# A difference of two activation blocks moved from DVE to POOL at the entry of the MLP

## The chip, the cores and the metric

The kernel runs on one core of a Trainium2 chip. A core has five engines that matter here: PE (the matrix engine; PEld is its loading of weights), DVE (VectorE), ACT (ScalarE), POOL (GpSimd) and SP, which only issues DMAs. Each runs its own queue of instructions in order, and they meet at semaphores. The metric is the device time of one execution in microseconds (us), the median of several.

## The reference: what is computed

One decoder layer with D_MODEL 1024, 512 tokens and one batch, all in float32: a modulated RMSNorm, two attention branches with gates and an output projection, then a second modulated RMSNorm `h2` and a gated MLP with a causal convolution, and a final RMSNorm. The change lies at the entry of the MLP:

```python
def _conv_ffn(h, w_up, conv_w, conv_b, w_down):
    u = h @ w_up
    a, g = jnp.split(u, 2, axis=-1)
    ...
    return (jax.nn.gelu(a, approximate=False) * g) @ w_down
```

`w_up` is 1024 x 5632 (two halves of 2816 columns), `h` is 512 x 1024.

## The kernel before

**A product in three matmuls.** A float32 matrix is used as a rounded high part and the low part that is left. ACT makes the high part (a cast), DVE the low part (source minus high part), and PE forms high x high, high x low and low x high. So each operand costs an ACT cast and a DVE subtraction before its matmuls can start.

**The MLP's first product by seven products.** `w_up` and the normalised input are cut into 2 x 2 blocks, and the eight block products are replaced by seven products of sums of blocks, in the manner of Strassen and Winograd. The kernel names them p1, m5, m6, p2, m7, p3 and p4. The blocks of the normalised, transposed input are `b11`, `b21`, `b12`, `b22`, each of 128 partitions x 4 x 256 (1024 float32 per partition). `b12` and `b22` are the two halves of one tile that the profile calls `braw`. The sums of input blocks that the products need are formed once: `t1n = b11 - b12`, then `t1n = -t1n - b22`, `b12 = b22 - b12` and `b21 = -t1n - b21`. Their high and low parts go to `tt[0]` to `tt[3]`, which the text calls t1 to t4 (tile `t` in the profile): `hi_t(i, ...)` is ACT's cast into `tt[i]`, L1275, and `lo_t(i, ...)` is DVE's subtraction, L1278. m5 uses t1, m6 uses t2, m7 uses t3 and p4 uses t4. p3 uses `b22` itself, whose high part is `bh[:, 2]` and whose low part is `bl[:, 2]` (L1407).

**The weights.** `w_up` is worked through in pairs of 128-column blocks, numbered J. For each J and each product, `sum_w` (DVE, L1087) forms the sum of weight blocks where m6 and p3 need one, `cast_w` (ACT, L1093) makes the high part `whi` and `low_w` (DVE, L1097) the low part `wlo`; three buffers of each kind go round. Some sums come from the DMA itself: SP issues the first load of a tile, and POOL issues a second load that adds to it (L1065). Raw loads go to SP's queue (L1063).

**The order around the change.** From the last steps of the output projection to the first slots of J = 2 the order of the instructions on PE, DVE, ACT and POOL is the order in which the program is written (a manual schedule); nothing is reordered by a planner. `mul_slot(J, name)` is 24 matmuls of one product (L1152), `behind(J, name)` takes its result out of PSUM: ACT copies for p1, m5 and m6, DVE additions for p2, m7 (L1192), p3 (L1194) and p4. `mod_one` (L1255 on DVE, L1257 on ACT) writes the blocks `b..` from the transposed rows with scale and shift. `conv_bias`, `conv_taps` (L1163, L1164) and `conv_gelu` are the convolution and its GELU. L1397 is the second form of `t1n`.

**POOL's queue here** holds four small powers for the RMSNorm (L173, of 128x1), then three adding loads of weights (one for J = 0, two for J = 1), and then the adding loads of later J; it does no other arithmetic in this stage.

Of the kernel before, what the change touches and what calls it, by code (L numbers as in the profile page):

```python
# [53 lines left out]
def kernel(  # L54
# [22 lines left out]
    nc = tc.nc  # L77
# [1055 lines left out]
    def psum(J, name):  # L1133
        if name in ("m5", "p3"):
            b, h = bV, J % 2
        elif name == "p2":
            b, h = bX, J % 2
        else:
            b, h = (bU0, bU1)[J % 2], J // 2 % 2
        return [b[u][:, h * H : (h + 1) * H] for u in range(2)]  # L1140
# [33 lines left out]
    def behind(J, name):  # L1174
        o = [] if name == "c22" else psum(J, name)
        g2 = g22[:, J % 2] if name in ("m5", "m7", "c22") else None
        if name == "p1":
            av[J] = big.tile([P, 2, S], F32, tag=("hhB", "hlB")[J % 2], name=f"a{J}")
        a = av[J]
        lo, hi = slice(0, H), slice(H, S)  # L1180
        for u in range(2):
            cc = grow(2 * J + u)
            if name == "p1":
                nc.scalar.copy(a[:, u, lo], o[u])
            elif name == "m5":
                nc.scalar.copy(g2[:, u], o[u])
            elif name == "m6":
                nc.scalar.copy(a[:, u, hi], o[u])
            elif name == "p2":
                nc.vector.tensor_add(a[:, u, lo], a[:, u, lo], o[u])  # L1190
            elif name == "m7":
                nc.vector.scalar_tensor_tensor(g2[:, u], g2[:, u], -1.0, o[u], ALU.mult, ALU.subtract)  # L1192
            elif name == "p3":
                nc.vector.tensor_add(a[:, u, hi], a[:, u, hi], o[u])  # L1194
            elif name == "p4":
                nc.vector.scalar_tensor_tensor(cc[:, lo], o[u], -1.0, cc[:, lo], ALU.mult, ALU.mult)
            elif name == "c22":
                nc.vector.tensor_mul(cc[:, hi], cc[:, hi], g2[:, u])
        if name == "p4":
            nc.vector.tensor_sub(grow(2 * J)[:, hi], grow(2 * J + 1)[:, hi], grow(2 * J)[:, hi])  # L1200
# [58 lines left out]
    def ks(g):  # L1259
        return slice(2 * (g % 2), 2 * (g % 2) + 2)  # L1260
# [13 lines left out]
    def hi_t(i, src, q=slice(0, 4)):  # L1274
        nc.scalar.copy(tt[i][:, 0, q], src[:, q])  # L1275
# [10 lines left out]
    V, q0, q1 = nc.vector, ks(0), ks(1)  # L1286
# [67 lines left out]
    b12, b22 = bt[:, 0], bt[:, 1]  # L1354
# [8 lines left out]
    def grow(j):  # L1363
        return gT[j // 4][:, j % 4]
# [31 lines left out]
    for q in (q0, q1):  # L1396
        V.scalar_tensor_tensor(t1n[:, q], t1n[:, q], -1.0, b22[:, q], ALU.mult, ALU.subtract)  # L1397
        hi_t(1, t1n, q)
    behind(0, "p1")
    nc.scalar.copy(bh[:, 2], b22)  # L1400
    low_w(0, "m6")
# [4 lines left out]
    cast_w(0, "p3")  # L1406
    V.tensor_sub(bl[:, 2], b22, bh[:, 2].bitcast(F32))  # L1407
    behind(0, "m5")
    V.tensor_sub(b12, b22, b12)
    hi_t(2, b12)  # L1410
    low_w(0, "p3")
    mul_slot(0, "p3")
# [404 lines left out]
```

## Time and profile before

| What | Value |
|---|---|
| median of 3 runs | 703.3 us (701.72 to 703.88) |
| profiled execution | 702.35 us, span 700.5 us |
| PE busy | 682.6 us, 97% of the span |
| DVE busy | 573.1 us, 82% |
| ACT busy | 375.1 us, 54% |
| POOL busy | 82.4 us, 12% |
| mean granted clock of PE | 0.995 |
| L1409 on DVE | 1 instruction of 1216 ns, at 378.8 us |

The span reaches from the first to the last instruction; the execution's time holds some 1.9 us more. Busy times are sums over the span and overlap between engines. A line such as L1409 is the line of the kernel before; a helper's line is shared by all its callers, so the time in the span tells which call it is.

### The profile page before, as it was taken

The numbers are of one execution on the slowest core, as the hardware profiler recorded it, in microseconds if no ns is written. First come the engines' busy times: TensorE is split into PE (matmuls) and PEld (weight loads), VectorE is DVE, ScalarE is ACT, GpSimd is POOL, SyncE is SP. The second block draws the span as 40 slices with busy tenths as digits, with TensorE's granted clock in tenths as the row PEclk, the third lists the DMA queues.
The fourth block names the chain that finished last, engine by engine and source line by source line (L and its number), as shares of the span: only waits on it lengthen the run. The fifth ranks groups of instructions, "written<-read, shape, count | busy, mean of one in ns | idle before, by whom it ended". The sixth has DMA issues, their size and how long they took to land.

```text
span 700.5 us, 11253 instructions
## 1 busy us (share of the span) xinstructions
PE 682.6 (97%) x4203; PEld 595.0 (85%) x4203; DVE 573.1 (82%) x1100; ACT 375.1 (54%) x666; POOL 82.4 (12%) x100
## 2 busy tenths in 40 slices
PE   6999999999999999999999999999999999999995
PEld 5777777777788888888889999999999999888884
DVE  5999886887985656663589999888888999979996
ACT  4646666454552333332468656655555666656664
POOL 3000000000001000000030111112111102540300
PEclk9999999999999999999999999999999999999998
DMA  9995454354535676239717788786889738997903
GB/s 313 289 273 159 149 152 151 98 173 121 140 102 160 207 232 185 91 99 281 251 39 144 151 200 199 174 209 184 209 213 217 173 129 219 191 198 196 166 1 120
DMA packets 115862, 121.81 MB, mean 174 GB/s; under 512 B 4383, under 2 KB 93280, under 8 KB 115808
## 3 DMA queue, kind: packets, MB, share of 16 engines
q1 hardware_dynamic: 96894, 95.09, 43.4%
q0 software_dynamic: 18720, 25.73, 22.0%
q8 instruction: 33, 0.54, 0.3%
q10 hardware_dynamic: 194, 0.28, 0.1%
q14 instruction: 21, 0.17, 0.1%
HBM read 118.97 MB, written 2.11 MB: 173 GB/s over the span
## 4 chain that ended last, share of the span: by engine, by line
PE 75%; DVE 13%; DMA 4%; ACT 4%; issue 2%; SPq 0%; POOL 0%; POOLq 0%; ACTq 0%
PE up L1152 26%; PE dc L1761 13%; DMA ra<-in_w_ada_dram 4%; PE a L332 3%; PE pgd L119 2%; PE oc L1208 2%; PE oc L1212 2%; PE pgd L121 2%; PE oc L1209 2%; PE pgd L120 2%; PE pga L119 2%; PE pga L121 2%; PE pga L120 2%; DVE arow L778 1%; DVE m_wlo L1097 1%
## 5 line engine op out<-in xcount | busy, mean ns | idle before, releaser
L1152 PE MATMUL up<-t,m_whi 128*128 128x256 f32 x528 | 96.2, 283 | 0.0
L1152 PEld LDWEIGHTS up<-t,m_whi 128*128 128x128 f32 x528 | 82.3, 192 | 0.0
L1152 PE MATMUL up<-t,m_wlo 128*128 128x256 f32 x264 | 74.7, 284 | 0.5 <-DVE m_wlo L1097 0.5
L1152 PE MATMUL up<-bh,p_wlo 128*128 128x256 f32 x232 | 65.6, 283 | 0.1
L1152 PE MATMUL up<-bh,p_whi 128*128 128x256 f32 x232 | 65.6, 283 | 0.0
L1152 PE MATMUL up<-bl,p_whi 128*128 128x256 f32 x232 | 65.6, 283 | 0.0
L778 DVE SCALAR_TENSOR_TENSOR arow<-ra,cs,arow 128x512 f32<-128x512 f32 x56 | 41.9, 749 | 21.0 <-DMA ra<-in_w_ada_dram 20.5
L1152 PEld LDWEIGHTS up<-t,m_wlo 128*128 128x128 f32 x264 | 50.6, 192 | 0.9 <-DVE m_wlo L1097 0.9
L1152 PEld LDWEIGHTS up<-bh,p_wlo 128*128 128x128 f32 x232 | 44.5, 192 | 0.3 <-DVE p_wlo L1097 0.3
L1152 PEld LDWEIGHTS up<-bl,p_whi 128*128 128x128 f32 x232 | 44.5, 192 | 0.0
L1152 PEld LDWEIGHTS up<-bh,p_whi 128*128 128x128 f32 x232 | 44.5, 192 | 0.0
L1065 POOL DMA_DIRECT2D s<-in_w_up_dram x21 | 27.0, 1360 | 143.1 <-DMA s<-in_w_up_dram 54.2
L1097 DVE TENSOR_TENSOR m_wlo<-s,m_whi 128x1024 fp32r<-128x1024 f32 x31 | 37.7, 1217 | 0.9 <-ACT m_whi L1093 0.9
L1093 ACT CAST m_whi<-s 128x1024 fp32r<-128x1024 f32 x31 | 32.4, 1047 | 9.6 <-DVE s L1087 6.2
L1152 PE MATMUL up<-t,p_whi 128*128 128x256 f32 x176 | 32.3, 284 | 0.5 <-DVE pairs L1192 0.5
L173 POOL TENSOR_TENSOR r<-ms,mhalf 128x1 f32<-128x1 f32 (+1 forms) x16 | 12.7, 796 | 133.1 <-DVE ms L171 74.1
L795 POOL DMA_DIRECT2D mod_rows<-row x8 | 5.1, 642 | 197.4 <-ACT row L794 197.4
L1152 PEld LDWEIGHTS up<-t,p_whi 128*128 128x128 f32 x176 | 27.4, 192 | 0.7 <-issue 0.7
L698 ACT ACTIVATE sd<-sd,dmx 128x128 f32<-128x128 f32 (+3 forms) x32 | 17.7, 557 | 19.0 <-DVE dmx L690 18.8
L1159 ACT ACTIVATE gT<-a,cv 128x512 f32<-128x512 f32 x22 | 17.7, 813 | 17.7 <-DVE a L1194 17.3
L1093 ACT CAST p_whi<-wa 128x1024 fp32r<-128x1024 f32 x18 | 18.7, 1041 | 12.0 <-PE up L1152 7.2
L1152 PE MATMUL up<-t,p_wlo 128*128 128x256 f32 x88 | 24.9, 283 | 0.0
(473 smaller groups left out, 2053.6 us busy)
## 6 DMA issues: line engine op xcount, KB each, us to landing
ra<-in_w_ada_dram SPq DMA_DIRECT2D x32, 512.0 KB, 3.9
wa<-in_w_up_dram SPq DMA_DIRECT2D x22, 512.0 KB, 4.0
s<-in_w_up_dram SPq DMA_DIRECT2D x21, 512.0 KB, 4.7
s<-in_w_up_dram POOLq DMA_DIRECT2D x21, 512.0 KB, 6.9
adaw<-in_w_ada_dram SPq DMA_DIRECT2D x16, 512.0 KB, 5.4
w<-in_w_in_dram SPq DMA_DIRECT2D x12, 512.0 KB, 3.9
a<-in_w_up_dram SPq DMA_DIRECT2D x11, 512.0 KB, 4.7
b<-in_w_down_dram SPq DMA_DIRECT2D x10, 512.0 KB, 3.8
```

The source lines that it names most:

```text
L119: nc.tensor.matmul(o, lh, rh, start=start, stop=False)
L120: nc.tensor.matmul(o, lh, rl, start=False, stop=False)
L121: nc.tensor.matmul(o, ll, rh, start=False, stop=stop)
L332: nc.tensor.matmul(acc6[i], lhs[:, i * P : (i + 1) * P], rhs[k], start=k == 0 and p == 0, stop=last and p == 2)
L698: exp = nc.scalar.activation(pm[m], pm[m], AF.Exp, bias=mx[:, m : m + 1], scale=slope, accum_out=lsum[:, m : m + 1])
L778: nc.vector.scalar_tensor_tensor(ac, r[:, a], cc, ac, ALU.mult, ALU.add)
L1065: nc.gpsimd.dma_start(dst, upblock(*blk), accum_op=ALU.add)
L1093: nc.scalar.copy(W[J, name][0], R[J, SRC[name]])
L1097: nc.vector.tensor_sub(lo, R[J, SRC[name]], hi.bitcast(F32))
L1152: nc.tensor.matmul(o[u], w[:, k, cu], b[:, k], start=name in ("p1", "m5", "p2") and k == 0 and x == 0, stop=k == 3 and x == 2, skip_group_ ...
L1159: nc.scalar.activation(grow(j), av[J][:, u], AF.Identity, bias=cv[:, 66 + j : 67 + j], scale=cv[:, 44 + j : 45 + j])
L1761: nc.tensor.matmul(bank2[u][:, sl], a[:, q, cu], b[:, q, sl], start=first_mm and x == 0, stop=last_mm and x == 2, skip_group_check=name no ...
```

## The change

The subtraction that forms `b12 = b22 - b12` is issued on POOL (`nc.gpsimd`) in place of DVE (`V` is `nc.vector`), and its place in the written order is earlier: behind the loop that forms the second `t1n`, ahead of the low weights of m6 and the weight sum of p3. Operands, shapes and result stay what they were. PE, ACT and SP keep their instructions and their order. ACT's cast `hi_t(2, b12)` now waits for POOL. In POOL's queue the new instruction stands behind the three adding loads for J = 0 and 1 and ahead of the first adding load for J = 2.

```diff
     for q in (q0, q1):
         V.scalar_tensor_tensor(t1n[:, q], t1n[:, q], -1.0, b22[:, q], ALU.mult, ALU.subtract)
         hi_t(1, t1n, q)
+    nc.gpsimd.tensor_sub(b12, b22, b12)
     behind(0, "p1")
     nc.scalar.copy(bh[:, 2], b22)
     low_w(0, "m6")
...
     cast_w(0, "p3")
     V.tensor_sub(bl[:, 2], b22, bh[:, 2].bitcast(F32))
     behind(0, "m5")
-    V.tensor_sub(b12, b22, b12)
     hi_t(2, b12)
     low_w(0, "p3")
     mul_slot(0, "p3")
```

## The prediction

> **What bounds the kernel now.** I read the page's busy shares first (PE 97%, DVE 82%, POOL 12%), then busy time by stretches around the edited line, then the list of waits there, then the chain of work that ended last, and at the end the timelines of DVE, ACT and POOL. The times below are microseconds from the start of the span. Busy time by stretches; after the length, the columns are PE, PEld, DVE, ACT, POOL (instructions in brackets), granted clock, DMA share, GB/s:
>
> ```profile
> 372.00:380.00 8.00, 8.00 (x69) 8.00 (x68) 8.00 (x11) 5.18 (x9) 0.00 (x0) 1.00 0.81 180
> 380.00:412.00 32.00, 30.99 (x252) 30.14 (x250) 30.85 (x43) 21.98 (x33) 5.10 (x4) 1.00 0.67 144
> 412.00:450.00 38.00, 37.94 (x316) 37.95 (x317) 33.88 (x51) 22.06 (x32) 5.13 (x4) 1.00 0.87 198
> ```
>
> DVE has no gap between 372 and 380, and about a microsecond in the next 32. PE loses its time in the second row only: from 412 on it is full (to 600 as well). So whatever DVE gains or loses between 372 and 412 reaches PE there, and PE carries it to the end unchanged. The waits of 372 to 412 name what PE waited for (engine, line, then what it waited on, us in total, times, longest):
>
> ```profile
> PE up L1152 <- DVE pairs L1192: 0.5, 1, 0.5
> PEld up L1152 <- DVE m_wlo L1097: 0.5, 1, 0.5
> ...
> PEld up L1152 <- DVE p_wlo L1097: 0.3, 1, 0.3
> ...
> PE up L1152 <- DVE m_wlo L1097: 0.3, 1, 0.3
> ```
>
> All are waits for DVE. Matmuls of this stage start 0.12 apart; at the four stalls the starts are 0.38 apart (380.80 to 381.18), 0.55 (384.03 to 384.58), some 0.77 (to 390.88) and, at 412.06, a wait of 0.20. That is 0.26 + 0.43 + 0.65 + 0.2, about 1.5 us: no relief of DVE here can give more. The removed subtraction and its neighbours on DVE (start, duration, line, out<-in):
>
> ```profile
> 371.75 1.29 DVE L1278 TENSOR_TENSOR t<-s_t,t 128x512 fp32r<-128x512 f32 x2
> 372.96 1.28 DVE L1397 SCALAR_TENSOR_TENSOR s_t<-s_t,braw 128x512 f32<-128x512 f32 x2
> 374.16 1.22 DVE L1097 TENSOR_TENSOR m_wlo<-s_t,m_whi 128x1024 fp32r<-128x1024 f32 x1
> ...
> 377.64 1.22 DVE L1407 TENSOR_TENSOR bl<-braw,bh 128x1024 fp32r<-128x1024 f32 x1
> 378.77 1.22 DVE L1409 TENSOR_TENSOR braw<-braw 128x1024 f32<-128x1024 f32 x1
> 379.91 1.22 DVE L1097 TENSOR_TENSOR p_wlo<-s_t,p_whi 128x1024 fp32r<-128x1024 f32 x1
> ```
>
> L1409 is the instruction that goes. Every DVE instruction shown reads two operands from SBUF, and each starts about 0.08 before its forerunner ends.
>
> **Part 1, DVE loses L1409.** Start to start it costs 379.91 - 378.77 = 1.14 us of an engine that has no gap. Without it p_wlo (L1097) ends at 379.99 instead of 381.13, and its matmul, due at 380.92, no longer waits. The second stall (m_wlo of m7, DVE end 384.53) is due 383.4 against a PE that comes at 383.9: gone. The third shrinks: DVE's end moves from 391.06 to 389.9, PE arrives at 389.5. What is late next is again DVE, at 412, where it is 1.14 earlier. Full worth: -1.1 us.
>
> **Part 2, POOL gains one subtraction of 128x1024.** Its order on POOL is behind three accumulating weight loads and ahead of the next one. The last of the three issues is over at 368.3; the next load is issued at 388.55, after a wait of 20.2 for a DMA. So nothing queued on POOL's queue notices an instruction of a few microseconds; SP's queue is not touched. The subtraction waits for DVE's L1383 (ended 369.4) and for ACT's last write of b22 (L1257, which ends at 371.84). It is ready at 371.9, not at 378.8.
>
> **Part 3, ACT's rounding of b12 (hi_t(2), L1275) waits for POOL instead of DVE.** ACT started it at 380.02 after 0.68 of idle time; ACT itself is free at 379.35. POOL therefore has 379.35 - 371.9 = 7.4 us of cover. Behind it on ACT stand the rounding of m7's weights, two copies of m6 and hi_t(3); they lose nothing as long as the cover holds, so this wait costs nothing. Past the cover each microsecond of POOL delays hi_t(2), then DVE's low part of t3 and m7's matmuls, one for one.
>
> **Part 4, POOL beside DVE.** The trace has no POOL subtraction, but has rows in which the two engines meet:
>
> ```profile
> 350.09 0.57 POOL L173 TENSOR_TENSOR r<-ms,mhalf 128x1 f32<-128x1 f32 x1 [28.44 <-DVE ms L171]
> 354.32 0.94 POOL L173 TENSOR_TENSOR r<-ms,mhalf 128x1 f32<-128x1 f32 x1 [3.67 <-DVE ms L171]
> ```
>
> ```profile
> 2.88 0.52 DVE L233 TENSOR_SCALAR cs<-cs 128x8 f32<-128x8 f32 x1 [2.02 <-ACT cs L232]
> ...
> 5.33 0.17 DVE L241 TENSOR_SCALAR cols<-cols 128x8 f32<-128x8 f32 x1
> ...
> 354.16 0.69 DVE L1293 TENSOR_TENSOR early<-wa,early 128x512 fp32r<-128x512 f32 x1
> ```
>
> ```profile
> 2.83 0.55 POOL L148 IOTA ddf<- 128x512 f32 x1
> 3.34 0.39 POOL L145 TENSOR_SCALAR_AFFINE_SELECT dsw<-dsw 128x256 f32<-128x256 f32 x1
> 3.70 0.61 POOL L149 TENSOR_SCALAR_AFFINE_SELECT ddf<-ddf 128x512 f32<-128x512 f32 x1
> ```
>
> The same POOL instruction takes 0.57 with DVE idle and 0.94 when it starts inside a DVE instruction with two SBUF inputs: it ends 355.26, which is 0.41 after DVE's end at 354.85. At 359.80 it does so again (0.40 after). The other way round, DVE's 128x8 at 2.88 took 0.52 instead of 0.17 and ended at 3.40, just after POOL's IOTA (2.83 to 3.38). So each can hold the other up to the other's end. At 695.25 POOL's power started in the first of two adjoining two-input DVE products (L1683, 695.03 and 695.36, 0.42 each) and ended at 695.85, 0.40 after the first: it was let in between the two. I therefore expect POOL to start at 372.43, when the first L1278 ends, and DVE's second L1278 to wait until POOL has read.
>
> How long is that? One-input selects give (607 - 395) ns / 256 = 0.83 ns per element, 0.85 us for 1024; a POOL instruction let in has 0.40 besides (above). Low end: both inputs stream at once, 0.40 + 0.85 = 1.25 us. High end: read, read and write one after the other, 0.40 + 2.55 = 2.95. I take the middle, two passes, 0.40 + 1.70 = 2.1 us: it is nearest to the selects, which read one operand and write one in 0.83 ns, with the second operand added. A lower end, no hold at all, is a rival below; the power rows (1.03 for 128x4 against 0.55: 0.16 us per element, 164 us for 1024) I leave out as the work of a power, with 2 in 100.
>
> The Trainium skill, GPSIMD Engine Reference, section "Performance versus the Vector engine", gives 4497 ns for a two-input add of 2048 elements; half of it is an estimate of 2.25 us, and the sum would be +1.1 instead of +1.0.
>
> DVE is thus 2.1 later from 372.43 and 2.1 - 1.14 = 1.0 later from L1409's place on. In between PE has slack: m5's matmuls start at 374.92 and need the second half of t1's low part only at the eighth (375.8; it comes at 375.1); m6 needs its first low half at 377.92, and gets it at 378.1 (375.98 + 2.1). p3 needs p_wlo, which comes at 382.1: PE restarts 1.0 later than before, and so at 384.58, 390.88 and 412.06.
>
> **Sum.** -1.14 + 2.1 = +1.0 us. The profiled execution took 702.35 (span 700.5 and 1.85 around it), 0.95 below the median of 703.3; 703.35 against its own time, 704.3 against the median. With the ends of part 4: +0.1 to +1.8, 703.4 to 705.1.
>
> **Rivals.**
> - *POOL does not hold DVE at all* (faster). For it: POOL's power of 128x4 (181.75 to 182.94) had DVE's two-input L704 start inside it at 182.61 and take its usual 0.61. Against it: that power has only four elements to read, and had read them. Decides if DVE's rows at 372 to 375 keep 0.68. Then part 1 alone: -1.1, 702.2.
> - *POOL is not let in* while DVE's two-input instructions follow each other without a gap. For it: there is no gap until DVE itself needs b12; against it: 695.25. DVE would run p_wlo and L1413 to 381.1 and stop; POOL 381.1 to 383.2, hi_t(2) to 384.3, low part of t3 to 385.5, m_wlo of m7 to 386.7 instead of 384.53: +2.2, and hi_t(3), behind two more ACT jobs, some 0.3 more. 705.5 to 705.8.
> - *POOL is much slower than its selects*, above 3.3 us, under DVE's traffic. Every microsecond of hold counts in full: 4 us gives +2.9, 706.2.
>
> By the Trainium skill, SBUF — State Buffer, section "Who interferes with whom", a VectorE instruction with two SBUF inputs and a GpSimd instruction that reads SBUF exclude each other for the whole instruction, and whichever issues first blocks the other. By that rule the forecast's hold is right and moving the work gives nothing; the trace shows the wait in both directions, but no long two-input POOL read.
>
> **How the numbers follow.** 0.3% (2.1 us) is about what a measurement of this kernel can tell from no change. Hold of about one subtraction: 0.50, mostly within 0.3%, 0.12 of it beyond for its upper end and the spread of the medians. Not let in: 0.22, on the bound, 0.17 of it beyond. Much slower POOL, the power's rate included: 0.12, all beyond. No hold: 0.16, 0.08 of it counted as beyond -0.3% because the medians' spread (701.72 to 703.88) can add a microsecond. Faster 0.08, same 0.51, slower 0.41. The range cuts the outer half of the no-hold case and the slowest POOL: 702.2 to 706.3; the likeliest case alone is 703.4 to 705.1.
>
> **What would show it.** POOL's L1399 starting at 372 to 372.5 and lasting 1.3 to 3; one DVE instruction near 372.4 (L1278 or L1397) stretched by as much; no L1409 on DVE; hi_t(2) starting near 381 without a wait for POOL; p_wlo's end at 382.1 relative to the same start; PE's wait before p3 over 1 us; PE full after 412. Wrong if the DVE rows beside POOL are unstretched (then faster), if POOL starts only at 381, or if PE loses time behind 412.

## The result, and the profile after

The changed kernel takes 703.95 us in the median of 19 runs (703.16 to 705.8), the kernel before 702.54 us in as many (701.72 to 704.57): a ratio of 1.0016, 95% interval 1.0008 to 1.0023. That is +1.1 us (0.6 to 1.6): less than the 0.3% that the prediction took for the least that can be told from no change, and still clear of no change, since there are 19 runs of each. The profiled execution of the changed kernel took 703.97 us with a span of 702.0 us, beside 702.35 and 700.5 before.

The profile after, busy time by stretches, same columns as before (PE, PEld, DVE, ACT, POOL, clock, DMA share, GB/s):

```profile
372.00:380.00 8.00, 7.84 (x65) 7.64 (x64) 8.00 (x9) 3.91 (x7) 2.77 (x1) 1.00 0.75 156
380.00:412.00 32.00, 30.67 (x249) 29.82 (x248) 30.86 (x43) 22.19 (x34) 5.13 (x4) 1.00 0.61 143
412.00:450.00 38.00, 37.80 (x315) 37.59 (x314) 33.88 (x49) 21.96 (x32) 5.13 (x4) 1.00 0.85 198
```

DVE is as full as it was and does less: 9 instructions in 372 to 380 in place of 11. POOL shows 2.77 us where it had none. The timelines of the changed kernel show where the time went (start, duration, line, out<-in). POOL's:

```profile
372.28 2.77 POOL L1399 TENSOR_TENSOR braw<-braw 128x1024 f32<-128x1024 f32 x1 [3.61 <-ACT braw L1257]
```

And DVE's:

```profile
372.11 3.50 DVE L1278 TENSOR_TENSOR t<-s_t,t 128x512 fp32r<-128x512 f32 x2
375.53 1.28 DVE L1397 SCALAR_TENSOR_TENSOR s_t<-s_t,braw 128x512 f32<-128x512 f32 x2
...
380.21 1.21 DVE L1408 TENSOR_TENSOR bl<-braw,bh 128x1024 fp32r<-128x1024 f32 x1
381.40 1.23 DVE L1097 TENSOR_TENSOR p_wlo<-s_t,p_whi 128x1024 fp32r<-128x1024 f32 x1
```

The pair of L1278 took 1.29 us before and takes 3.50 now: +2.21. Taken singly, the first ran 372.11 to 372.79 as ever, and the second 372.71 to 375.61, 0.56 after POOL's end at 375.05. POOL was ready inside the first and got in behind it; the second then waited until POOL was done. L1409 is gone, so from the first L1278 to p_wlo's start it is 9.29 us (372.11 to 381.40) against 8.16 before (371.75 to 379.91): +1.13. PE's timeline of the changed kernel, what it waited for in the last brackets:

```profile
378.60 0.38 PE L1152 MATMUL up<-t,m_whi 128*128 128x256 f32 x1 [0.16 <-DVE t L1278]
...
382.68 0.39 PE L1152 MATMUL up<-bh,p_wlo 128*128 128x256 f32 x1 [0.49 <-DVE p_wlo L1097]
...
386.09 0.39 PE L1152 MATMUL up<-t,m_wlo 128*128 128x256 f32 x1 [0.28 <-DVE m_wlo L1097]
...
392.38 0.47 PE L1152 MATMUL up<-t,p_whi 128*128 128x256 f32 x2 [0.49 <-DVE pairs L1192]
```

The last two waits are those of before, of the same length; the first is new and the second longer. The first matmul of m5 and the last stall, before:

```profile
374.92 0.40 PE L1152 MATMUL up<-t,m_whi 128*128 128x256 f32 x2
...
412.06 0.38 PE L1152 MATMUL up<-t,m_wlo 128*128 128x256 f32 x1 [0.20 <-DVE m_wlo L1097]
```

The same two, after:

```profile
375.28 0.40 PE L1152 MATMUL up<-t,m_whi 128*128 128x256 f32 x2
...
413.54 0.39 PE L1152 MATMUL up<-t,m_wlo 128*128 128x256 f32 x1 [0.20 <-DVE m_wlo L1097]
```

From the one to the other PE needed 412.06 - 374.92 = 37.14 us before and 413.54 - 375.28 = 38.26 now: +1.12, and after it PE is full in both. The rest of the two spans' difference of 1.5 us, 0.36, stood already at m5's first matmul, ahead of the change's place; it belongs to these two executions and not to the change.

ACT's rounding of b12 was never late. ACT's timeline of the changed kernel:

```profile
380.32 1.05 ACT L1093 CAST p_whi<-s_t 128x1024 fp32r<-128x1024 f32 x1 [1.36 <-DVE s_t L1087]
381.28 0.63 ACT L1186 COPY pairs<-up 128x256 f32<-128x256 f32 x2
381.80 1.06 ACT L1275 CAST t<-braw 128x1024 fp32r<-128x1024 f32 x1
```

L1275 has no idle time in front of it (0.68 before): b12 had been ready since 375.05.

### The profile page after: what moved, and what is told of

It reads as the page before. It is cut to its first block, busy times and chain, and to the rows that moved or that the text cites. A ratio compares the mean times of both kernels' runs of the same rounds, so it can differ in the third digit from the quotient of the medians.

```text
span 702.0 us, 11254 instructions
## 1 busy us (share of the span) xinstructions
PE 682.4 (97%) x4203; PEld 593.5 (85%) x4203; DVE 574.3 (82%) x1099; ACT 374.9 (53%) x666; POOL 85.2 (12%) x101
## 4 chain that ended last, share of the span: by engine, by line
PE 74%; DVE 15%; DMA 5%; ACT 3%; issue 2%; SPq 0%; POOL 0%; POOLq 0%; ACTq 0%; DVEq 0%
PE up L1152 26%; PE dc L1761 13%; DMA ra<-in_w_ada_dram 3%; PE a L332 2%; PE pgd L119 2%; PE oc L1208 2%; PE oc L1212 2%; PE pgd L120 2%; PE pgd L121 2%; PE oc L1209 2%; PE pga L119 2%; PE pga L121 2%; PE pga L120 2%; DVE m_wlo L1097 1%; DVE arow L778 1%
## 5 line engine op out<-in xcount | busy, mean ns | idle before, releaser
L1097 DVE TENSOR_TENSOR m_wlo<-s,m_whi 128x1024 fp32r<-128x1024 f32 x31 | 37.7, 1217 | 0.9 <-ACT m_whi L1093 0.9
```

The costliest lines, as they stand in the source:

```text
L1097: nc.vector.tensor_sub(lo, R[J, SRC[name]], hi.bitcast(F32))
```

## Experiments

The theory: the removed DVE instruction is worth about 1.1 us, and POOL's subtraction costs DVE the time for which POOL reads SBUF, about 2.2 us, because DVE's next instruction reads two operands from SBUF. Rivals: the cost is ACT's new wait or the moved order; it is a fixed price of each meeting; any POOL instruction, or any DVE instruction, is affected. Where not said otherwise, an edit is made to the kernel before.

**Each half of the change alone.** First the subtraction on no engine, so that b12 goes on unsubtracted:

```diff
-    V.tensor_sub(b12, b22, b12)
```

> The kernel before without the subtraction b12 = b22 - b12 on any engine (b12 goes on unsubtracted, so that part of the computation is left out; everything else is as before). It measures what the removed DVE instruction is worth alone. Hold theory (DVE's 1.14 us comes back, POOL's hold takes 2.2): about -1.1 us against before, PE waits before p3 and m7 gone, PE full after 412. Rival (the change is slower because something other than the hold was lost, and the removal is worth little): within 0.3 us of before.

Measured: 701.46 us against 702.38, ratio 0.9988 (0.9978 to 0.9997), so -0.8 us (-1.5 to -0.2). The times alone reach into the rival's 0.3 us; the trace decides below. Between m5 and 412 PE waits only twice, for `pairs` (0.3) and for `m_wlo` (0.2). Then the opposite, DVE's subtraction kept and a second one on POOL whose result nobody reads:

```diff
         hi_t(1, t1n, q)
+    nc.gpsimd.tensor_sub(fgb.rearrange("p (k n) -> p k n", n=256), b22, b12)
     behind(0, "p1")
```

> The kernel before with its DVE subtraction kept, and a POOL subtraction of the same two operands into a buffer that nobody reads, at the changed kernel's place. It measures the hold alone. Hold theory: one DVE L1278 at 372 stretched by about 2.2 us, +2.2 us against before, no wait of ACT for POOL. Rival (ACT's new wait for POOL, or the moved order, is what costs): no change, since nobody waits for this POOL instruction.

Measured: 704.33 us against 702.38, ratio 1.0028 (1.0018 to 1.0038), so +2.0 us (1.3 to 2.7). The timeline of DVE in this kernel:

```profile
371.40 3.50 DVE L1278 TENSOR_TENSOR t<-s_t,t 128x512 fp32r<-128x512 f32 x2
...
380.64 1.21 DVE L1410 TENSOR_TENSOR braw<-braw 128x1024 f32<-128x1024 f32 x1
381.77 1.22 DVE L1097 TENSOR_TENSOR p_wlo<-s_t,p_whi 128x1024 fp32r<-128x1024 f32 x1
```

And its longest wait of PE (us in total, times, longest):

```profile
PE up L1152 <- DVE p_wlo L1097: 1.6, 1, 1.6
```

The same 3.50 us, although no engine waits for this POOL instruction. So neither ACT's new wait nor the moved order is the cause; the meeting itself is. The halves add up: -0.8 + 2.0 = +1.2, and the change measured +1.1.

**What of POOL's work holds DVE.** POOL writes the idle buffer and reads nothing:

```diff
+    nc.gpsimd.memset(fgb, 0.0)
```

> The kernel before with a POOL memset of 128x1024 float32 into the same idle buffer at the same place in POOL's queue: it writes 1024 elements per partition and reads none. If POOL's reads are what holds DVE's two-input instructions: DVE rows beside it keep 0.68 and 1.22 us. If any long POOL instruction that writes SBUF holds them: one DVE row stretched by the memset's length, some 0.9 us.

One profiled run, 702.46 us. POOL in this kernel's timeline:

```profile
366.90 2.57 POOL L1399 MEMSET fgbr<- 128x1024 f32 x1
```

And DVE beside it:

```profile
368.34 1.28 DVE L1383 TENSOR_TENSOR s_t<-braw,braw 128x512 f32<-128x512 f32 x2
```

The memset needs no data and so started at 366.90, beside the issues of the adding loads (364.57 to 368.51), and ended at 369.47. The only two-input work of DVE in that span, the pair of L1383, kept its 1.28; the next, L1097, starts after it. When within its span the memset wrote can't be read from this, so it says less than the next one, a copy with one input:

```diff
+    nc.gpsimd.tensor_copy(fgb.rearrange("p (k n) -> p k n", n=256), b22)
```

> The kernel before with a POOL copy of b22 (128x1024 float32, one input) into the idle buffer at the same place. If the hold lasts as long as POOL reads, and two operands are read one after the other: a DVE row stretched by about half of the changed kernel's 2.2 us, 1.0 to 1.3. If the hold is a fixed price of meeting: 2.2 again. If one input holds nothing: 0.

One run, 702.54 us. POOL in this kernel's timeline:

```profile
371.33 1.43 POOL L1399 COPY fgbr<-braw 128x1024 f32<-128x1024 f32 x1 [3.58 <-ACT braw L1257]
```

And DVE beside it:

```profile
371.18 2.13 DVE L1278 TENSOR_TENSOR t<-s_t,t 128x512 fp32r<-128x512 f32 x2
```

The pair took 0.84 us more than its 1.29, a little under the 1.0 to 1.3 expected. A copy holds DVE too, and for less than half of the subtraction's 2.21: 0.82 ns per element against 2.16. The price is no fixed one, and a subtraction costs more than twice a copy. Whether that lies in the second operand alone is not shown, since the operation differs too. Nor do the runs separate POOL's reading from the whole of its instruction; only the memset bears on that, and weakly. Half of the subtraction, as an additional instruction:

```diff
+    nc.gpsimd.tensor_sub(fgb.rearrange("p (k n) -> p k n", n=256)[:, q0], b22[:, q0], b12[:, q0])
```

> The kernel before with its own subtraction kept and a POOL subtraction of the first 512 columns only, into the idle buffer, at the same place. Hold theory: one DVE row near 372 stretched by 1.1 us, half of the 2.2 of the full one, and some +1 us at the end, less what slack there is before p3. Rival (fixed price): 2.2 again.

It became ready a little earlier and met L1087 in place of L1278:

```profile
371.32 2.27 DVE L1087 TENSOR_TENSOR s_t<-s_t,wa 128x1024 f32<-128x1024 f32 x1
```

That is 2.27 us instead of 1.22, so +1.05, about half of 2.21 as expected. The one run took 703.99 us, 1.6 over the median before; by its time alone one run can't be told from the +1 expected. Then the changed kernel's subtraction in two halves:

```diff
-    nc.gpsimd.tensor_sub(b12, b22, b12)
+    for q in (q0, q1):
+        nc.gpsimd.tensor_sub(b12[:, q], b22[:, q], b12[:, q])
```

> The changed kernel with POOL's subtraction in two halves of 128x512, one behind the other. Hold theory (DVE waits for as long as POOL reads, 2.2 ns per element): the stretch of DVE's rows is 2.2 us in sum again, perhaps in two rows of 1.1 if DVE gets in between the halves; the time stays at some +1.1 us over before. Rival (a fixed price for each meeting of the two engines): the stretch doubles to 4.4, +3.3 us.

DVE's timeline in this kernel:

```profile
370.65 2.26 DVE L1087 TENSOR_TENSOR s_t<-s_t,wa 128x1024 f32<-128x1024 f32 x1
372.83 2.38 DVE L1278 TENSOR_TENSOR t<-s_t,t 128x512 fp32r<-128x512 f32 x2
```

Two rows are stretched, by 1.04 and 1.09, 2.1 in sum: DVE and POOL take turns, and twice as many meetings cost no more. One run took 703.62 us, +1.2 over before.

**Which DVE work is held.** An additional POOL subtraction, ready when DVE has a gap and then two instructions that read PSUM:

```diff
+    nc.gpsimd.tensor_sub(fgb.rearrange("p (k n) -> p k n", n=256), b21, bl[:, 1].bitcast(F32))
     load_s3(0)
```

> The kernel before with an additional POOL subtraction of 128x1024 (b21 minus the low part of p2's block, into an idle buffer) that becomes ready some 5 us earlier, when DVE has nothing to do for 0.6 us and then two instructions that read PSUM and no block from SBUF (L1255), before its next two-input instruction (L1383). If only DVE instructions with two SBUF inputs are held: POOL starts at about 366.7, both L1255 rows keep 0.54 us beside it, and the first L1383 is stretched to POOL's end at about 369, by some 0.7 us and not 2.2. If any DVE instruction is held by POOL's reads: L1255 stretched by 1.5 to 2 us. The three adding loads behind it on POOL are issued some 3 us later, which may cost something at m7.

The timeline of POOL in this kernel:

```profile
366.58 2.40 POOL L1356 TENSOR_TENSOR fgbr<-braw,bl 128x1024 f32<-128x1024 f32 x1 [2.73 <-DVE bl L1272]
```

And of DVE:

```profile
367.25 1.00 DVE L1255 TENSOR_SCALAR braw<-th,c 128x256 f32<-128x256 f32 x2 [0.75 <-ACT braw L1257]
368.17 1.96 DVE L1384 TENSOR_TENSOR s_t<-braw,braw 128x512 f32<-128x512 f32 x2
```

Both L1255 ran their usual 0.54 each (1.00 for the pair) in the middle of POOL's 2.40; the two-input pair behind them took 1.96 instead of 1.28, +0.68, when POOL had 0.81 left at its start. POOL work of the same size that cost DVE 2.2 us at 372 cost it 0.7 here. In these traces, then, DVE instructions with two SBUF operands wait for POOL, and L1255, which reads its block from PSUM, did not; this last is seen in this trace alone. A DVE instruction that reads one block from SBUF met no POOL subtraction in any run, so that case stays open. The run took 703.11 us beside 702.28 of one run before.

**Whether the place decides.** m6's first weight sum (s1 + a11), a DVE instruction of the same 1.14 us in the full stretch, is formed early instead, ahead of the last split of the output weights, in a buffer that is free by then; once by DVE, once by POOL:

```diff
     lo_early(1, slice(0, 4))
+    ES[0, "m6"] = ES[0, "p3"] = raw_tile([P, 4, 256], "early_m6")
+    V.tensor_add(ES[0, "m6"], R[0, "s1"], R[0, "a11"])      # or nc.gpsimd.tensor_add
...
-    sum_w(0, "m6")
...
-    sum_w(0, "p3")
+    V.tensor_add(ES[0, "p3"], ES[0, "p3"], R[0, "a12"])
```

`cast_w` and `low_w` read this buffer for m6 and p3 of J = 0.

> The kernel before, with m6's first weight sum (s1 + a11, one DVE instruction of 1.14 us in the full stretch at 371) formed by DVE some 25 us earlier, ahead of the last split of the output weights, into a raw buffer that is free by then; p3's sum goes on from that buffer. The same subtraction of b12 stays on DVE. Theory (a DVE microsecond taken out of 368 to 390 is worth a PE microsecond, and before 347 DVE has idle time): -0.8 to -1.1 us against before, like the kernel without the subtraction, if the split of the last output weights is not late. Rival (the early place costs PE what the late one gains): 0.

> As the kernel with m6's first weight sum formed early, but POOL forms it: a POOL addition of 128x1024 in the stretch of 340 to 350 in place of DVE's 1.14 us at 371. Theory (the hold costs only where DVE is the bound): a DVE row stretched by up to 2.2 us near 342 to 346, hidden by DVE's idle time there but for some tenths, and the full gain of 1.14 later: -0.3 to -1.1 us. Rival (work given to POOL costs wherever it runs): +1 us, as the changed kernel.

DVE: 701.21 us against 702.39, ratio 0.9983 (0.9973 to 0.9992), -1.2 us. POOL: 701.15 us, ratio 0.998 (0.9971 to 0.9989), -1.4 us. The two can't be told apart; both are faster than the kernel before and the changed one, and both gained a little more than the 0.8 to 1.1 and 0.3 to 1.1 expected. In the POOL version, the timeline of DVE around the new place:

```profile
341.63 3.25 DVE L116 TENSOR_TENSOR early<-wa,early 128x1024 fp32r<-128x1024 f32 x1 [0.31 <-ACT early L115]
344.81 1.21 DVE L116 TENSOR_TENSOR wo_l<-wo,wo_h 128x1024 fp32r<-128x1024 f32 x1
347.31 1.28 DVE L1223 TENSOR_TENSOR x<-x,oc 128x512 f32<-128x512 f32 x2 [1.29 <-PE oc L1217]
```

That of POOL:

```profile
341.42 2.38 POOL L1303 TENSOR_TENSOR early_m<-s_t,wa 128x1024 f32<-128x1024 f32 x1 [20.35 <-DMA a<-in_w_up_dram]
```

And all that PE waits for from 300 to 420, in the list of waits:

```profile
PE up L1157 <- DVE m_wlo L1102: 0.2, 1, 0.2
```

The same POOL work on the same amount of data holds DVE here too (3.25 us instead of 1.22), and PE loses nothing by it that shows: DVE is idle for 1.29 us before 347.31 all the same, and PE waits 0.2 us in all between 300 and 420, as in the version on DVE. The rival that POOL's work costs wherever it runs has fallen.

**The same stretch of PE in every kernel.** Five of these kernels ran once, and single times scatter by more than what is sought. But each trace has the stretch that was used above, from m5's first matmul to the stall of 0.20 for `m_wlo` near 412, behind which the list of waits shows none for PE up to the end of the span. The last column is what DVE's own rows gave: the lengthening of its rows less 1.14 for an instruction that is gone from the stretch (all in us).

| Kernel | m5's first matmul | last stall | between | against before | by DVE's rows |
|---|---|---|---|---|---|
| before | 374.92 | 412.06 | 37.14 | | |
| changed | 375.28 | 413.54 | 38.26 | +1.12 | +1.07 |
| subtraction on no engine | 373.88 | 409.94 | 36.06 | -1.08 | -1.14 |
| additional subtraction on POOL | 374.58 | 413.92 | 39.34 | +2.20 | +2.21 |
| memset on POOL | 375.10 | 412.23 | 37.13 | -0.01 | 0 |
| copy on POOL | 374.34 | 412.33 | 37.99 | +0.85 | +0.84 |
| half of a subtraction, additional | 375.63 | 413.81 | 38.18 | +1.04 | +1.05 |
| changed, in two halves | 374.96 | 413.16 | 38.20 | +1.06 | +0.99 |
| additional subtraction, 5 us earlier | 374.93 | 412.73 | 37.80 | +0.66 | +0.68 |
| first sum early, on DVE | 375.06 | 410.93 | 35.87 | -1.27 | -1.14 |
| first sum early, on POOL | 374.66 | 410.53 | 35.87 | -1.27 | -1.14 |

What DVE gained or lost reached PE within 0.13 us in every kernel, the copy and the half subtraction included, where the single times (+0.2 and +1.6) don't show it. The kernel with the subtraction 5 us earlier also issued its adding loads later; up to here that cost nothing beside the 0.68.

## Why the prediction was right

The forecast was +1.0 us, 704.3 against the median then known (703.3), with 703.4 to 705.1 for the likeliest case; measured +1.1 and 703.95. With 19 runs the kernel before came out at 702.54, 0.8 below the median that the 704.3 stands on, so the two changes are the better comparison. The case it gave most weight, a hold of about one subtraction, is what happened.

- *Part 1*, L1409 worth 1.14 us: DVE's row went, and without the instruction on any engine the kernel gained 0.8 (0.2 to 1.5), somewhat under the step's value but with it inside the interval; PE's stretch in that trace is 1.08 shorter. The stall at `pairs` stayed at 0.3, as the step allowed.
- *Part 2*, ready at 371.9 and nobody behind it on POOL's queue: POOL started at 372.28 in a stretch that ran 0.36 late, so at 371.92 on the old scale; the next adding load again waited for a DMA (14.90 us).
- *Part 3*, 7.4 us of cover: b12 came at 375.05 and ACT needed it at 381.80.
- *Part 4*, the hold: it was expected at the end of the first L1278, on the second, and was there. Its size was 2.21 against 2.1. The working behind the 2.1 was wrong in two places that cancel, and that it came so near is luck: it had 0.40 of fixed time and 0.83 ns for each operand and element. The half and the halved subtraction show no fixed part to speak of (1.05 and 2.1), and the copy shows 0.82 ns for one operand but the subtraction 2.16 ns for two. The figure of the Trainium skill (GPSIMD Engine Reference, section "Performance versus the Vector engine"), worked out to an estimate of 2.25 us for this size, was nearer than the rows of the trace of before. POOL subtractions and sums of this size that no DVE instruction kept waiting took 2.40 and 2.38 in the profile.
- *The slack between*: m6 was said to get its first low half 0.2 us late and p3 to wait over 1 us. The starts show PE losing 0.32 at m6 (378.16 to 378.60, less 0.12), 0.24 at p3's first matmul (381.33 to 381.69) and 0.65 at its third, against 0.26 there before: 0.95 in sum. The sum was right; it fell in three stalls where one was announced, so the announced wait of over 1 us before p3 did not show. The 0.24 came by a path that the prediction left out: p3's first matmul waited for ACT's copy `pairs` (L1186 at 381.28), which stands behind ACT's cast of p3's weights, and that cast had waited 1.36 us for DVE's L1087.
- *The rivals*: POOL not holding DVE at all is refuted by the 3.50. POOL not let in is refuted too: in every run in which POOL's operands were ready while DVE's two-input instructions followed each other without a gap, it got its turn behind the one that ran. A much slower POOL: 2.8 us from start to end here, not 3.3 or more.
- *The Trainium skill*, SBUF — State Buffer, section "Who interferes with whom": the rule on two-input VectorE instructions and GpSimd reads now has its long read. The stretch of 2.21 beside a POOL subtraction, 0.84 beside a copy, and none for L1255 agree with it.
- *A row that does not fit*: for a DVE that waits for POOL the prediction had the instruction at 2.88 (0.52 instead of 0.17). It has one operand, and the IOTA beside it reads nothing, so it is not the case of two operands that the runs show. What made it 0.35 us longer than L241 of the same size stays open; the conclusion drawn from it was right all the same.

## What to carry to other kernels

An elementwise instruction moved from a full DVE to an idle POOL is not free because POOL is idle: in these runs POOL's two-input subtraction of 128x1024 kept DVE's two-input instructions waiting for 2.2 us and spared DVE 1.14. Before such a move, look at what DVE runs at the moment at which POOL's operands are ready: the part of POOL's work that ran beside instructions that read PSUM cost nothing, and where DVE had idle time a sum on POOL cost PE nothing that showed. When one stretch is bound by an engine, the better question is which of its work has its inputs long before; one sum moved some 30 us earlier shortened PE's stretch by 1.27 us, on DVE as on POOL, so the gain came from the place and not from the engine.

## What was not expected of the hardware

A copy of 1024 elements per partition held DVE for 0.84 us, a subtraction of two such blocks for 2.21: 2.6 times as long, where two operands read one after the other at the copy's rate would take twice as long. And in the run with two halves the two engines alternated: the first half went ahead of L1087 (370.65, stretched by 1.04), L1087 then ran to 372.91, and the second half went ahead of the first L1278 (372.83, 1.78 us instead of 0.68). In that run neither engine waited for more than one instruction of the other, though DVE had no gap to offer.
